# The order of the three products of a split matrix multiply: all column tiles in each pass

## The chip, the cores and the metric

The kernel runs on one core of a Trainium2 chip. TensorE (PE) multiplies, VectorE (DVE) and ScalarE (ACT) work elementwise, GpSimd (POOL) and SyncE (SP) issue most of the DMAs. The metric is the device time of one execution in microseconds; the timed runs are repeated, and their median counts.

## What is computed

Two transformer blocks over 256 tokens of width 2048, all in float32. The first has a sparse attention with compressed, selected and windowed keys and a gated feed-forward layer; the second has a sliding-window attention beside a latent attention, a squared-ReLU feed-forward layer, and scales and shifts that come from a vector `c`. Cut to the products with large weights:

```
h = rmsnorm(x);  proj = h @ nsa_w_in;  x = x + attention(proj) @ nsa_w_out
z = rmsnorm(x) @ ffn_w_in;  x = x + (silu(z[:, :5632]) * z[:, 5632:]) @ ffn_w_out;  x = rmsnorm(x)
mod = silu(c) @ w_mod + b_mod          # six vectors: sh1, sc1, g1, sh2, sc2, g2
h = rmsnorm(x) * (1 + sc1) + sh1;  proj = h @ w_in   (also w_uq, w_ukv)
x = x + g1 * (concat(window(proj), latent(proj)) @ w_out)
h = rmsnorm(x) * (1 + sc2) + sh2
x = x + g2 * (relu(h @ w_ff1) ** 2 @ w_ff2);  return rmsnorm(x)
```

## The kernel before

**Tiles and splitting.** Activations lie feature-major, 16 tiles `xs` of 128 features by 256 tokens (`S`). Each float32 value is split into a high half (rounded to the engine's fp32r form) and a low half, the rest: `split` (L83) has ACT write the high half (L84) and DVE the low half (L85). An activation tile holds both, `xt[:, 0, :]` high and `xt[:, 1, :]` low; they are made by `scaled` (L672 on ACT, L673 on DVE), `modulated` (L931, L933, L934) or `split`. A product of two split numbers is three products on TensorE: high x high, high x low, low x high (`mm3`, L125 to L129, weights first). The weights are the stationary operand, x the moving one, 256 columns wide.

**`gemm` (L131)** multiplies a block of weight columns by all x tiles. The columns are `nm` tiles of 128; each has half a PSUM bank, so a bank (`acc`, four of them in turn) holds two column tiles. Weights come in pieces of `kk` x tiles (`w_cols`): SP loads a piece into `raw` (five buffers), ACT and DVE split it into `whi` and `wlo` (four buffers each). The loop runs over the pieces, over the x tiles k of a piece, and over the column tiles m, and for each m writes the three products one after the other. At the end `evac` empties the banks: L642 adds to `h` (two tiles of `h` at once), L1086 does the same with a scale, one tile at a time. `gemm_tok` (L153) and `gemm_tok2` (L192) are the token-major forms with the weights as the moving operand; they have their own products.

**How wide.** Most gemms are 512 columns wide (`nm` = 4, two banks). `nsa_w_out` (L1036) runs as two gemms of eight column tiles, four banks each. `w_out_2` (L1092) runs as gemms of 8, 4, 2, 1 and 1 column tiles (`WIDE`), and the last part of `ffn_w_out` of 4, 4, 4, 2, 1 and 1 (`GROUPS`).

**What sets the order.** The code is written in program order, and a scheduler lays out each engine's instructions by its own estimate of when operands are ready. Attention heads are written between gemms, so their small matmuls (names `S`, `PT`, `O`; L588 to L629 in the first block, L952 to L1006 in the second) come to stand among the products of the gemm beside them. The vector `mod` is worked out on DVE in the background (`macc`, L742, a step after each piece; four one-row matmuls at L723), with its loads `mw` on POOL's queue, paced by the product that was written last (`self.last`).

Of the kernel before, what the change touches and what calls it, by code (L numbers as in the profile page):

```python
# [17 lines left out]
S = 256  # L18
# [48 lines left out]
class Kernel:  # L67
# [63 lines left out]
    def gemm(self, w, ld, row, xs, cols, evac, kk=2, order=None):  # L131


        n = sum(c for _, c in cols)
        nm, nk = n // 128, len(xs)
        acc = [self.bank("acc", 4) for _ in range((nm + 1) // 2)]
        order = order or list(range(0, nk, kk))
        done = 0
        for k0 in order:
            c = min(kk, nk - k0)  # L140
            hi, lo = self.w_cols(w, ld, row + 128 * k0, c, cols)
            for k in range(c):
                xt = xs[k0 + k]
                done += 1
                for m in range(nm):
                    self.mm3(acc[m // 2][:, (m % 2) * S:(m % 2 + 1) * S],
                             hi[:, k, m * 128:(m + 1) * 128], lo[:, k, m * 128:(m + 1) * 128],
                             xt[:, 0, :], xt[:, 1, :], done == 1 and m % 2 == 0, done == nk)
            self.step(c * nm / 64)
        for i, b in enumerate(acc):  # L150
            evac(i, b)
# [1040 lines left out]
```

## Time and profile before

| what | us |
|---|---|
| median of the timed runs | 2122.26 |
| fastest and slowest of the three | 2120.37, 2122.82 |
| the profiled execution | 2119.85 |
| its span, first to last instruction | 2118.0 |
| PE busy | 2094.1 |
| weight loads (PEld) busy | 1992.5 |
| DVE busy | 1452.0 |
| ACT busy | 1017.1 |

The profiled execution is one of its own, so its span is not the span of a timed run. PE's products are pipelined: one lasts 0.28 us from its start to its end, and the next starts before it has ended. The busy time of PE is the union of these, so it says that PE had something in it and not how fast products followed each other; that is read from the starts in the timeline, or from the number of products in a stretch. A stretch counts each instruction that overlaps it. Stages by time: norm, projections and compressed keys to about 200 us, the first attention to 357, `nsa_w_out` to 420, the first feed-forward layer to 1150, the second block's projections and attention to 1355, `w_out_2` to 1400, the second feed-forward layer to the end.

### The profile page before, as it was taken

The page shows a single profiled execution, that of the slowest core. Times are in us where ns is not written, and L with a number is a line of the kernel's source. Part 1 is how long each engine was busy: PE and PEld are TensorE (multiplying, and loading weights), DVE is VectorE, ACT ScalarE, POOL GpSimd, SP SyncE. Part 2 cuts the span into 40 slices and gives each one's busy share as a digit, 9 for nine tenths or more (in the row PEclk, how much of TensorE's full clock was granted, in tenths as well). Part 3 has the DMA queues.
Part 4 walks back from the last instruction along what each step waited for, and adds up shares of the span by engine and source line. Part 5 has one row for each costly group of instructions (what it writes and reads, how often), then busy time and mean ns, then how long its engine had stood idle before and what let it go on. Part 6 is the DMA issues. An engine that isn't in the chain of part 4 may idle for free. (4 is left out here: it accounts for less than half of the span.)

```text
span 2118.0 us, 40943 instructions
## 1 busy us (share of the span) xinstructions
PE 2094.1 (99%) x16405; PEld 1992.5 (94%) x16405; DVE 1452.0 (69%) x2144; ACT 1017.1 (48%) x1504; POOL 162.9 (8%) x297
## 2 busy tenths in 40 slices
PE   9999999999999999999999999999999999999998
PEld 8899999999999999999999999899889989989987
DVE  7467876787777777877867676677676555555556
ACT  6334655554434434443445465565434534534543
POOL 2211000010110111101000000000100000000000
PEclk9999999999999999999999999999999999999999
DMA  8778555889889888888975663568887656656663
GB/s 277 261 234 311 170 163 180 286 265 296 276 282 303 274 301 281 279 294 276 298 233 156 182 183 112 160 196 280 283 294 233 194 191 194 193 193 193 192 194 133
DMA packets 288302, 492.29 MB, mean 232 GB/s; under 512 B 27111, under 2 KB 139338, under 8 KB 287856
## 3 DMA queue, kind: packets, MB, share of 16 engines
q1 hardware_dynamic: 254128, 371.20, 55.2%
q0 software_dynamic: 33408, 117.70, 16.7%
q8 instruction: 128, 2.10, 0.4%
q10 hardware_dynamic: 576, 0.79, 0.1%
q14 instruction: 62, 0.51, 0.1%
HBM read 487.21 MB, written 2.20 MB: 231 GB/s over the span
## 5 line engine op out<-in xcount | busy, mean ns | idle before, releaser
L84 ACT ACTIVATE whi<-raw 128x1024 fp32r<-128x1024 f32 (+2 forms) x716 | 746.2, 1044 | 904.8 <-PE acc L128 645.4
L85 DVE TENSOR_TENSOR wlo<-raw,whi 128x1024 fp32r<-128x1024 f32 (+2 forms) x716 | 853.5, 1200 | 392.1 <-ACT whi L84 378.8
L127 PE MATMUL acc<-x,whi 128*128 128x256 f32 x3184 | 882.6, 278 | 3.2 <-ACT v L463 1.4
L128 PE MATMUL acc<-x,whi 128*128 128x256 f32 x3184 | 884.3, 278 | 0.0
L129 PE MATMUL acc<-x,wlo 128*128 128x256 f32 x3184 | 882.7, 278 | 0.2 <-DVE wlo L85 0.2
L127 PEld LDWEIGHTS acc<-x,whi 128*128 128x128 f32 x3184 | 597.8, 188 | 8.6 <-issue 5.0
L128 PEld LDWEIGHTS acc<-x,whi 128*128 128x128 f32 x3184 | 599.4, 188 | 5.4 <-issue 4.6
L129 PEld LDWEIGHTS acc<-x,wlo 128*128 128x128 f32 x3184 | 599.0, 188 | 1.4 <-DVE wlo L85 0.6
L742 DVE SCALAR_TENSOR_TENSOR macc<-mw,csil,macc 128x1024 f32<-128x1024 f32 x180 | 231.1, 1284 | 175.0 <-DMA mw<-w_mod 174.1
L128 PE MATMUL acc<-u,whi 128*128 128x256 f32 x1260 | 349.7, 279 | 0.8 <-DVE u L85 0.8
L127 PE MATMUL acc<-u,whi 128*128 128x256 f32 x1260 | 346.3, 280 | 1.0 <-DVE h L642 0.6
L129 PE MATMUL acc<-u,wlo 128*128 128x256 f32 x1260 | 347.0, 278 | 0.0
L128 PEld LDWEIGHTS acc<-u,whi 128*128 128x128 f32 x1260 | 236.7, 188 | 1.9 <-DVE u L85 1.5
L127 PEld LDWEIGHTS acc<-u,whi 128*128 128x128 f32 x1260 | 234.9, 188 | 3.2 <-ACT u L84 1.0
L129 PEld LDWEIGHTS acc<-u,wlo 128*128 128x128 f32 x1260 | 235.9, 188 | 0.7 <-issue 0.2
L164 PE MATMUL acc<-whi,u 128*128 128x512 f32 (+1 forms) x544 | 206.2, 379 | 0.0
L165 PE MATMUL acc<-wlo,u 128*128 128x512 f32 (+1 forms) x544 | 206.1, 379 | 0.0
L163 PE MATMUL acc<-whi,u 128*128 128x512 f32 (+1 forms) x544 | 204.4, 376 | 0.0
L736 POOL DMA_DIRECT2D mw<-w_mod x192 | 102.6, 534 | 1003.2 <-PE acc L129 657.7
L164 PEld LDWEIGHTS acc<-whi,u 128*128 128x128 f32 x544 | 102.2, 188 | 20.6 <-issue 0.4
L163 PEld LDWEIGHTS acc<-whi,u 128*128 128x128 f32 x544 | 102.1, 188 | 20.3
L165 PEld LDWEIGHTS acc<-wlo,u 128*128 128x128 f32 x544 | 102.2, 188 | 18.4
(349 smaller groups left out, 1316.9 us busy)
## 6 DMA issues: line engine op xcount, KB each, us to landing
raw<-w_ff SPq DMA_DIRECT2D x256, 512.0 KB, 4.1
mw<-w_mod POOLq DMA_DIRECT2D x192, 512.0 KB, 5.6
raw<-ffn_w_in SPq DMA_DIRECT2D x352, 256.0 KB, 5.0
raw<-ffn_w_out SPq DMA_DIRECT2D x87, 512.0 KB, 5.3
raw<-nsa_w_in SPq DMA_DIRECT2D x72, 512.0 KB, 5.3
raw<-nsa_w_out SPq DMA_DIRECT2D x32, 512.0 KB, 4.5
raw<-w_out SPq DMA_DIRECT2D x32, 512.0 KB, 4.0
raw<-w_in SPq DMA_DIRECT2D x24, 512.0 KB, 3.9
```

Source lines behind the costliest of these rows:

```text
L84: self.nc.scalar.activation(hi, x, AF.Copy)
L85: self.nc.vector.tensor_tensor(lo, x, hi.bitcast(F32), OP.subtract)
L127: mm(out, wh, xh, start=first, stop=False, skip_group_check=True)
L128: mm(out, wh, xl, start=False, stop=False, skip_group_check=True)
L129: self.last = mm(out, wl, xh, start=False, stop=last, skip_group_check=True)
L163: mm(o, xt[:, 0, q], hi, start=k == 0, stop=False)
L164: mm(o, xt[:, 1, q], hi, start=False, stop=False)
L165: self.last = mm(o, xt[:, 0, q], lo, start=False, stop=k == nk - 1)
L736: ld = nc.gpsimd.dma_start(wt, self.src(self.a["w_mod_2"], k * 128 * LD + s * 1024, [[LD, 128], [1, 1024]]))
L742: nc.vector.scalar_tensor_tensor(acc, wt, csil[:, k:k + 1], acc, op0=OP.mult, op1=OP.add)
```

## The change

The loop over column tiles moves inside a loop over the three passes. For one x tile, the first pass runs high weights x low x over all column tiles, the second high x high, the third low x high. The order of the three is other than before (high x high was first). The first product of a bank still opens it, the last pass of the last x tile closes it. `gemm_tok` and `gemm_tok2` stay as they are, and so does `mm3`, which `w_ukv` still calls. Names of lines from here on are two higher in the changed kernel (L642 is L644 there), and all the moved products have line L147.

```
-                for m in range(nm):
-                    self.mm3(acc[m // 2][:, (m % 2) * S:(m % 2 + 1) * S],
-                             hi[:, k, m * 128:(m + 1) * 128], lo[:, k, m * 128:(m + 1) * 128],
-                             xt[:, 0, :], xt[:, 1, :], done == 1 and m % 2 == 0, done == nk)
+                for i, (wt, j) in enumerate(((hi, 1), (hi, 0), (lo, 0))):
+                    for m in range(nm):
+                        self.last = self.nc.tensor.matmul(
+                            acc[m // 2][:, (m % 2) * S:(m % 2 + 1) * S], wt[:, k, m * 128:(m + 1) * 128], xt[:, j, :],
+                            start=done == 1 and i == 0 and m % 2 == 0, stop=done == nk and i == 2,
+                            skip_group_check=True)
```

PE in the first attention, around the transposes of one head (`PT` from `sb_2326`; `O` is the head's output). Before:

```order
L129 MATMUL acc<-x,wlo 128x256
L127 MATMUL acc<-x,whi 128x256
L620 MATMUL PT<-ident,sb_2326 128x128 x4
L128 MATMUL acc<-x,whi 128x256
L129 MATMUL acc<-x,wlo 128x256
L127 MATMUL acc<-x,whi 128x256
L626 MATMUL O<-pt,vcc 128x256
L128 MATMUL acc<-x,whi 128x256
L129 MATMUL acc<-x,wlo 128x256
```

The same place in the changed kernel:

```order
L147 MATMUL acc<-x,wlo 128x256 x4
L147 MATMUL acc<-x,whi 128x256 x8
L622 MATMUL PT<-ident,sb_2326 128x128 x4
L628 MATMUL O<-pt,vcc 128x256
L147 MATMUL acc<-x,wlo 128x256 x4
L147 MATMUL acc<-x,whi 128x256 x8
```

The eight products of the two high passes now stand together and the four low ones behind them; the three products between the head's two steps have moved away from there, so that the gemm is broken into once and not twice.

DVE at the end of the first gemm of `nsa_w_out`, where the four banks are added to `h` and the next x tiles are scaled. Before:

```order
L742 SCALAR_TENSOR_TENSOR macc<-mw,csil,macc 128x1024
L85 TENSOR_TENSOR wlo<-raw,whi 128x1024
L642 TENSOR_TENSOR h<-h,acc 128x512
L85 TENSOR_TENSOR wlo<-raw,whi 128x1024
L742 SCALAR_TENSOR_TENSOR macc<-mw,csil,macc 128x1024
L642 TENSOR_TENSOR h<-h,acc 128x512 x2
L673 SCALAR_TENSOR_TENSOR x<-h,vec_821,x 128x256
L642 TENSOR_TENSOR h<-h,acc 128x512
L673 SCALAR_TENSOR_TENSOR x<-h,vec_821,x 128x256
```

The same place in the changed kernel:

```order
L744 SCALAR_TENSOR_TENSOR macc<-mw,csil,macc 128x1024
L85 TENSOR_TENSOR wlo<-raw,whi 128x1024 x2
L744 SCALAR_TENSOR_TENSOR macc<-mw,csil,macc 128x1024
L644 TENSOR_TENSOR h<-h,acc 128x512 x4
L85 TENSOR_TENSOR wlo<-raw,whi 128x1024
L675 SCALAR_TENSOR_TENSOR x<-h,vec_821,x 128x256 x2
```

The four additions, which stood among a weight split, a `macc` step and a scaling, now stand in one row behind the `macc` step.

## Rows read from the trace of the kernel before

**Rows 1.** The page's head and busy times: us, share of the span, instructions.
```profile
span 2118.0 us, 40943 instructions
...
PE 2094.1 (99%) x16405; PEld 1992.5 (94%) x16405; DVE 1452.0 (69%) x2144; ACT 1017.1 (48%) x1504; POOL 162.9 (8%) x297
```

**Rows 2.** Waits of PE: who waited for whom, us in total, times, longest.
```profile
PE acc L127 <- DVE h L642: 1.3, 2, 0.7
...
PE acc L128 <- DVE u L85: 0.8, 2, 0.7
...
PE acc L129 <- DVE wlo L85: 0.2, 1, 0.2
```

**Rows 3.** Timeline of PE, feed-forward stretch: start us, duration us, instruction.
```profile
500.29 0.28 PE L127 MATMUL acc<-x,whi 128*128 128x256 f32 x1
500.40 0.28 PE L128 MATMUL acc<-x,whi 128*128 128x256 f32 x1
500.51 0.28 PE L129 MATMUL acc<-x,wlo 128*128 128x256 f32 x1
500.63 0.28 PE L127 MATMUL acc<-x,whi 128*128 128x256 f32 x1
```

**Rows 4.** PE in stretches: stretch, length, PE busy (instructions), granted clock, DMA share, GB/s.
```profile
460.00:530.00 70.00, 70.00 (x620) 1.00 0.92 299
...
1357.00:1397.00 40.00, 40.00 (x342) 1.00 0.61 180
```

**Rows 5.** The page's costliest groups: count | busy us, mean ns | idle before.
```profile
L128 PE MATMUL acc<-x,whi 128*128 128x256 f32 x3184 | 884.3, 278 | 0.0
...
L128 PE MATMUL acc<-u,whi 128*128 128x256 f32 x1260 | 349.7, 279 | 0.8 <-DVE u L85 0.8
```

**Rows 6.** Timeline, DVE and PE, middle of `nsa_w_out`; in brackets the idle time before.
```profile
376.60 1.28 DVE L742 SCALAR_TENSOR_TENSOR macc<-mw,csil,macc 128x1024 f32<-128x1024 f32 x1 [1.14 <-DMA mw<-w_mod]
...
377.63 0.28 PE L128 MATMUL acc<-u,whi 128*128 128x256 f32 x1
377.80 1.28 DVE L642 TENSOR_TENSOR h<-h,acc 128x512 f32<-128x512 f32 x2
...
378.54 0.39 PE L127 MATMUL acc<-u,whi 128*128 128x256 f32 x1 [0.63 <-DVE h L642]
```

**Rows 7.** Timeline, DVE and PE, end of `nsa_w_out`.
```profile
419.92 0.68 DVE L642 TENSOR_TENSOR h<-h,acc 128x512 f32<-128x512 f32 x1
...
420.75 0.36 PE L127 MATMUL acc<-x,whi 128*128 128x256 f32 x1 [0.67 <-DVE h L642]
```

**Rows 8.** Timeline of DVE, end of the eight-wide gemm of `w_out_2`.
```profile
1353.79 3.23 DVE L1086 SCALAR_TENSOR_TENSOR h<-acc,modc,h 128x256 f32<-128x256 f32 x8 [0.95 <-PE acc L129]
```

**Rows 9.** Timeline of PE at the same place.
```profile
1355.23 0.28 PE L129 MATMUL acc<-u,wlo 128*128 128x256 f32 x1
...
1355.38 0.36 PE L127 MATMUL acc<-u,whi 128*128 128x256 f32 x1
```

**Rows 10.** Timeline, first gemm of the second block's projections.
```profile
1154.25 0.80 PE L127 MATMUL acc<-x,whi 128*128 128x256 f32 x2 [1.12 <-ACT x L933]
...
1154.89 0.58 PE L128 MATMUL acc<-x,whi 128*128 128x256 f32 x1
```

**Rows 11.** Timeline, first gemm of the second feed-forward layer.
```profile
1406.77 0.49 PE L127 MATMUL acc<-x,whi 128*128 128x256 f32 x2
...
1407.28 0.38 PE L128 MATMUL acc<-x,whi 128*128 128x256 f32 x1
```

**Rows 12.** Timeline of PE, products after a break in the first attention.
```profile
304.74 0.47 PE L129 MATMUL acc<-x,wlo 128*128 128x256 f32 x1
305.05 0.28 PE L127 MATMUL acc<-x,whi 128*128 128x256 f32 x1
```

**Rows 13.** Timeline of PE at the lower clock, first gemm of the kernel.
```profile
9.54 0.41 PE L128 MATMUL acc<-x,whi 128*128 128x256 f32 x1
...
10.18 0.41 PE L129 MATMUL acc<-x,wlo 128*128 128x256 f32 x1
```

## The prediction, made before the changed kernel ran

> **What bounds the kernel now.** I read the page's head first: the span is 2118.0 us, PE is busy 2094.1 us of it, DVE 1452.0 and ACT 1017.1 [rows 1]. So TensorE is the bound from end to end, and a busy share of 99% may still hide a poor pace. The waits come next, and PE hardly has any: two waits for a bank come to 1.3 us, two for a low half to 0.8, one for `wlo` to 0.2 [rows 2]. The weights' splits are always early. Then the pace itself. In the feed-forward stretch the timeline shows one product starting every 0.113 us, whatever follows what: L127 to L128 (same output, same weights, the other half of x), L128 to L129 (same output, other weights), L129 to L127 (other output, other weights, same half of x) [rows 3]. Over whole stretches the counts say the same. A stretch counts about two instructions more than start in it, because a product lasts 0.28 us and those begun earlier count too: 70 us / 618 = 113.3 ns, but 40 / 340 = 117.6, both at full granted clock [rows 4]. So there are two paces, 113.3 and 117.7 ns. By the starts in the timeline the slow one holds four long stretches (38.3 to 59.4, 172.9 to 189.9, 1355.6 to 1400.6, 1583.1 to 1597.6 us, some 830 products) and about as many again in short pieces of the attention stages: 1,650 x 4.4 ns = 7.3 us. The lines that the change touches make 3 x (3184 + 1260) = 13,332 products [rows 5]; one nanosecond on each would be 13.3 us.
>
> **The steady part: 0.** Nothing is removed or added: the same 13,332 products, with as many weight loads, over the same operands. What changes is which product follows which. Of the new neighbours, "other output, other weights, same half of x" makes ten of twelve steps with four column tiles; in the other two the half or the tile of x changes as well. It stands in the trace before as L129 to L127, at 0.113 us like the two others [rows 3]. The weights of a column tile were loaded twice in a row before (L127, L128) and are loaded four loads apart now; the trace shows no saving on the second of the two, so none is lost. I take 0, and the two paces as the bounds of what can happen (rivals below). `hi` is read to the end earlier and `lo` is needed later, by six products (0.7 us) in a piece of four tiles. ACT and DVE get that as slack; it is worth the one `wlo` wait, -0.2 us [rows 2].
>
> **Where the sum is: the ends of gemms eight tiles wide.** Before, the column tiles of the last k finish one after the other, three products each, so a bank (two tiles) is done every 0.68 us and DVE can empty it while PE works on. Now all tiles finish in the third pass, and the four banks are done 0.23 us apart, the first only six products before the end. The next gemm takes the same four banks, and now asks for all of them within its first pass. There are three such places.
> (a) Inside `nsa_w_out`, first to second half. Before, the last bank's add is late because DVE does `macc` first (376.60, 1.28 us) and then adds of 0.64 us; PE waits once, from about 377.85 to 378.54 [rows 6]. In the new order the four adds stand in a row behind `macc`. From 377.88 they end at 378.5, 379.1, 379.8 and 380.4; the first pass then ends near 380.7, not at 378.76 as without a wait: 1.9 us lost against 0.7, so +1.2. Were `macc` not in front, the adds begin at 377.4 and it is +0.75.
> (b) `nsa_w_out` to the feed-forward's first gemm, which takes two banks. Before, PE waits for the first (419.92 to 420.75) [rows 7]; now the second ends 0.64 us after the first while its turn comes 0.23 us after: +0.4 (0.2 to 0.6).
> (c) `w_out_2`, eight tiles to four. Before, no wait: DVE's eight updates take 3.23 us from 1353.79, 0.40 each, two to a bank [rows 8], and PE goes straight from 1355.23 to 1355.38 [rows 9]. Now the first bank is done at 1355.23 - 6 x 0.118 + 0.28 = 1354.8 and is empty at 1355.65, the second at 1356.45: PE loses 0.3 and then 0.6 us: +0.9 (0.6 to 1.2). The gemms of one and two tiles after it take other banks or end as before.
> Elsewhere two of the four banks serve a gemm of four tiles, and the next one takes the other two: a later release is hidden behind a whole gemm, and would cost up to 0.45 us per gemm without that.
>
> **The low half of x comes first now.** ACT writes the high half of an activation, DVE the low half after it. Before, PE could start with high x high. At 1154.25 and at 1406.77 it does two products so and then waits for DVE's L934 until 1154.89 and 1407.28 [rows 10, 11]. Now the first product waits for that: two products at 0.11 to 0.28 us each, 0.4 us each time, +0.8 together (0.4 to 1.2). In the second attention PE's order before has eleven places where four products of L127 run ahead of the low half. Each could cost up to 4 x 0.113 = 0.45 us, 5.0 us in all, or nothing where other matmuls fill it. Only two waits for `u`'s low half stand in the trace [rows 2], so I take two of them, +1.0 (0 to 5.0).
>
> **The order around it.** The scheduler moves the attention's small matmuls too. Counted over the whole of PE's order, runs of these products are broken into by other work 145 times before and 135 times now. A break shows its price where a product is followed after 0.31 us instead of 0.11 (304.74 to 305.05) [rows 12]: 0.2 us, and by the starts around other breaks 0.1 or hardly any. Ten fewer: -1.5 (-3.0 to 0). SP's queue keeps its order word for word, so no load moves.
>
> **Sum.** 0 - 0.2 + 1.2 + 0.4 + 0.9 + 0.8 + 1.0 - 1.5 = +2.6 us. The profiled execution took 2119.85 us (its span plus 1.85), so this gives 2122.45 for it; the median of the timed runs is 2122.26, and with the same 2.6 us on it the forecast is **2124.9 us**, 0.12% longer. With all terms at their low or high ends it is 2121.0 to 2131.5. About 0.2%, 4.2 us, is what a measurement of this kernel can tell from no change, so the bounds are 2118.0 and 2126.5.
>
> **Rivals.**
> 1. *The slow pace holds more of the products* (slower). Where: after each break the first products run at 117.7 ns, and something later drops PE to 113.3; in four long stretches it did not. If the new sequence of loads and products never drops out, the price is 4.4 ns x 11,700 = 51 us, 2176 us; a quarter of that gives 2138. It decides from some 360 products more than now (1.6 us to the bound). For: both paces come from something in the rhythm that the order could touch. Against: within each pace all three neighbours cost alike.
> 2. *PE's clock falls because the bank changes at every second product* (slower). Row first: from 460 to 530 us the bank changes at every sixth product and the granted clock is 1.00 [rows 4]; at the lower level products start 0.21 us apart (9.54 to 10.18) [rows 13]. The change triples the bank changes. If one product in twenty fell to the lower level, it would cost 667 x 0.1 = 67 us: 2192 us. The Trainium skill, "TensorE: Matmul & The Clock Gate", section "A second HAM failure mode: psum-queue depth-cycling", tells of a kernel that cycles through PSUM banks and whose clock swings between its levels, because PE idles a little between groups. By that rule this change would be slower; the trace so far speaks against it, since L129 to L127 changes the output without a gap.
> 3. *The slow pace goes away* (faster): -7.3 us on the sum, 2117.6.
> 4. *The waits at the starts do not arise*, because the scheduler fills them: without (a) to (c) and the low-half terms the sum is -1.7, 2120.6: no change that could be measured.
>
> **How the numbers follow.** Forecast 0.55 (within 0.2%: 0.38, slower 0.17); rival 1 0.12, slower; rival 2 0.04, slower; rival 3 0.17 (faster 0.10, same 0.07); rival 4 0.12 (same 0.10, faster 0.02). Together: faster 0.12, same 0.55, slower 0.33. The range 2114 to 2137 leaves out rival 2 (0.04), rival 1 beyond 8 us or so (0.08) and the far end of rival 3 (0.04).
>
> **What would show it.** In the new profile: products of the new line 113.3 ns apart in the feed-forward stretch, and counts per stretch that give 113.3 or 117.7 and nothing else; waits of PE for `h` of 1 to 2 us at the middle of `nsa_w_out` and some 0.9 us at the end of the eight-wide part of `w_out_2`; waits for the low half of x at the two stage starts; no wait for `wlo`. I am wrong if the pace in the long stretches is another number, if the granted clock falls inside them, or if the waits of PE grow by more than 6 us.

## The result, and the profile of the changed kernel

| | before | changed |
|---|---|---|
| median, us (12 runs each) | 2122.54 | 2133.22 |
| lowest to highest, us | 2119.65 to 2126.97 | 2127.50 to 2145.05 |
| profiled execution, us | 2119.85 | 2137.10 |
| its span, us | 2118.0 | 2135.2 |
| PE busy, us | 2094.1 | 2102.6 |

The changed kernel is slower: 1.0053 times the time of before, 95% interval 1.0041 to 1.0065, or some 11 us. That lies inside the range of 2114 to 2137, but outside the forecast's own case: +2.6 us was forecast, and "within 0.2%" was the likeliest sign. The profiled execution of the changed kernel is 4 us above its median; a second one (last experiment) took 2131.76 us, and I read both.

The page of the changed kernel: the head, the busy times, and the costliest groups of the new line (count | busy us, mean ns | idle us before it). They answer to [rows 1, 5].

```profile
span 2135.2 us, 40964 instructions
...
PE 2102.6 (98%) x16405; PEld 2001.0 (94%) x16405; DVE 1450.1 (68%) x2144; ACT 1016.3 (48%) x1504; POOL 163.0 (8%) x297
...
L147 PE MATMUL acc<-x,whi 128*128 128x256 f32 x6368 | 877.6, 279 | 5.7 <-ACT v L465 2.4
...
L147 PE MATMUL acc<-x,wlo 128*128 128x256 f32 x3184 | 502.7, 279 | 0.0
```

The instruction counts of the engines are those of before, so nothing was added. The new line waits 5.7 us where L127 waited 3.2. PE's waits in the changed kernel (us in total, times, longest), which answer to [rows 2]:

```profile
PE acc L147 <- DVE h L644: 2.8, 2, 1.6
PE acc L147 <- ACT v L465: 2.4, 1, 2.4
PE PT L967 <- DVE sb L964: 2.2, 2, 1.7
PE acc L147 <- DVE x L936: 2.1, 2, 1.8
PE S L725 <- DVE macc L744: 1.7, 3, 1.3
PE acc L147 <- DVE u L85: 1.7, 2, 0.9
```

Other lines of this list are left out. The same list of before has the waits for `h` (1.3), `v` (1.4), `sb` (0.7), `macc` (0.4) and `u` (0.8), and 1.1 for the high half of an activation where the low half stands now. The wait for `wlo` is gone. Added up between its first and last product, PE is idle 14.6 us before and 22.5 us after.

Two sums over PE's product starts explain most of the rest. Products at the slow pace (115 to 120 ns to the next) are 1731 before and 2901 now: 1170 x 4.4 ns = 5.1 us. Products at the lower of the two clock levels, 0.21 us apart [rows 13], are 23 before and 68 now: 45 x 0.1 = 4.5 us. Without these two, PE's busy time is 2094.1 - 7.6 - 2.3 = 2084.2 us before and 2102.6 - 12.8 - 6.8 = 2083.0 now. So 8.0 + 5.1 + 4.5 - 1.2 = 16.4 of the 17.2 us between the two spans; the other 0.8 stand behind PE's last instruction.

The slow pace is seen in stretches of the trace (stretch, its length, PE busy and instructions, granted clock, DMA share, GB/s). The changed kernel:

```profile
460.00:530.00 70.00, 70.00 (x620) 1.00 0.92 293
990.00:1084.00 94.00, 94.00 (x801) 1.00 0.87 277
```

The first has the count of before to the last product [rows 4]: the new order runs at 113.3 ns there. The second is 94 / 799 = 117.6 ns, in the same loop, with the granted clock at 1.00. Before, the same 94 us held 833 instructions.

### The profile page after: what moved, and what is told of

Read it like the earlier page. It is cut to its first block, busy times and chain, and to the rows that moved or that the text cites. A ratio compares the mean times of both kernels' runs of the same rounds, so it can differ in the third digit from the quotient of the medians.

```text
span 2135.2 us, 40964 instructions
## 1 busy us (share of the span) xinstructions
PE 2102.6 (98%) x16405; PEld 2001.0 (94%) x16405; DVE 1450.1 (68%) x2144; ACT 1016.3 (48%) x1504; POOL 163.0 (8%) x297
## 5 line engine op out<-in xcount | busy, mean ns | idle before, releaser
L147 PE MATMUL acc<-x,whi 128*128 128x256 f32 x6368 | 877.6, 279 | 5.7 <-ACT v L465 2.4
L147 PEld LDWEIGHTS acc<-x,whi 128*128 128x128 f32 x6368 | 796.7, 189 | 15.6 <-issue 11.4
L147 PE MATMUL acc<-x,wlo 128*128 128x256 f32 x3184 | 502.7, 279 | 0.0
L147 PEld LDWEIGHTS acc<-x,wlo 128*128 128x128 f32 x3184 | 427.3, 189 | 1.1 <-issue 0.6
L147 PE MATMUL acc<-u,whi 128*128 128x256 f32 x2504 | 346.8, 279 | 3.4 <-DVE u L85 1.7
L147 PEld LDWEIGHTS acc<-u,whi 128*128 128x128 f32 x2504 | 313.9, 188 | 5.9 <-DVE u L85 2.4
L147 PE MATMUL acc<-u,wlo 128*128 128x256 f32 x1252 | 200.6, 278 | 0.0
L147 PEld LDWEIGHTS acc<-u,wlo 128*128 128x128 f32 x1252 | 168.6, 188 | 0.3
L578 ACT ACTIVATE sb<-sb,nm 128x128 f32<-128x128 f32 (+4 forms) x144 | 59.2, 413 | 35.8 <-DVE nm L575 35.6
L575 DVE CUSTOM_DVE_ANT_0 sb<-S,bt 128x128 f32<-128x128 f32 (+3 forms) x128 | 33.2, 308 | 3.4 <-PE S L986 1.3
```

Source lines behind the costliest of these rows:

```text
L147: self.last = self.nc.tensor.matmul(acc[m // 2][:, (m % 2) * S:(m % 2 + 1) * S], wt[:, k, m * 128:(m + 1) * 128], xt[:, j, :], start=done ...
L575: r = nc.vector.tensor_tensor_reduce(sb[:, c], s, b, 1.0, 3e38, OP.add, OP.min, nm[:, i:i + 1])
L578: nc.scalar.activation(sb[:, c], sb[:, c], AF.Exp, bias=nm[:, i:i + 1], scale=-1.0, accum_out=sums[:, i:i + 1])
```

## Experiments

Each has the median of its runs and its ratio to runs of before on the same chip, with the 95% interval. Line numbers in waits move with each edit. Theory A: the loss stands at the ends of gemms, where banks are finished together and the next gemm asks at once for all of them and for the low half. Theory B: it stands in the inner order, by way of the slow pace. Theory C, from experiment 5 on: any new order costs in proportion to how much it moves. Theories D, E, P and Q, on the slow pace, stand in the expectations of experiments 9 to 11.

**1. Both ends undone.** The changed kernel, with the first and last x tile of each gemm in the old order:

```diff
+                if done in (1, nk):
+                    for m in range(nm):
+                        self.mm3(acc[m // 2][:, (m % 2) * S:(m % 2 + 1) * S],
+                                 hi[:, k, m * 128:(m + 1) * 128], lo[:, k, m * 128:(m + 1) * 128],
+                                 xt[:, 0, :], xt[:, 1, :], done == 1 and m % 2 == 0, done == nk)
+                    continue
                 for i, (wt, j) in enumerate(((hi, 1), (hi, 0), (lo, 0))):
```

> The changed kernel with the first and the last x tile of every gemm back in the old order (three products for a column tile, then the next tile, high x high first); all x tiles between keep the three passes. Theory A (the loss is at the ends of gemms: banks released late, low half of x asked for first, and the lower clock that follows such gaps): PE idle between its first and last product back from 22.5 us to about 15, no wait for h over 0.8 us, time as before, ratio 0.999 to 1.0015. Theory B (the order inside the gemm holds more products at the slow pace of 117.7 ns): about 2900 products at that pace as in the changed kernel against 1730 before, +5 us, ratio 1.002 to 1.004.

Measured: 2121.8 us, 1.001 [0.9994, 1.0026]. The loss is gone, as far as this interval can tell, with the passes still in all x tiles between. PE's idle time in the profile is 16.0 us; one wait for `h` of 1.4 us stayed, where I had expected none over 0.8.

**2. The ends alone.** The complement: `if 1 < done < nk:` in the place of `if done in (1, nk):`.

> The complement: only the first and the last x tile of every gemm run in three passes, all between in the old order. Theory A: nearly the whole loss, PE idle about 22 us, waits for h of 1 to 2 us, at the lower clock 5 to 10 us more than before, ratio 1.003 to 1.005. Theory B: idle may grow, but the slow pace stays at about 1700 products, ratio 1.001 to 1.0025.

Measured: 2131.3 us, 1.0046 [1.003, 1.0062]: nearly the whole loss from the two end tiles of each gemm. PE's idle time is 23.9 us and 1477 products are slow, fewer than before. Theory B, that the inner order sets the loss, falls with these two.

**3. High half first.** The changed kernel with the first two passes exchanged:

```diff
-                for i, (wt, j) in enumerate(((hi, 1), (hi, 0), (lo, 0))):
+                for i, (wt, j) in enumerate(((hi, 0), (hi, 1), (lo, 0))):
```

> The changed kernel with the passes in the order high x high, high x low, low x high. Theory A: the waits for the low half of x and u (2.1 and 1.7 us in the changed kernel) go or halve, the waits for h stay, so 2 to 3 us less than the changed kernel, ratio 1.003 to 1.004. Theory B: the passes are as long as before, ratio 1.005 as the change, some 2900 products at the slow pace.

Measured: 2128.6 us, 1.0033 [1.0022, 1.0043]. PE's wait for the low half at the second block's first gemm became the old one of 1.1 us for the high half; the waits for `h` stayed at 3.0 us. The passes cost some 7 us without the low half's help. In this one profile, whose time is that of the median, little of it is idle time (17.1 us, 2.5 more than before) and more is the slow pace (3688 products, 8.6 us more).

**4. Low half first, in the old order.** The kernel before, with the first two products of `mm3` exchanged:

```diff
-        mm(out, wh, xh, start=first, stop=False, skip_group_check=True)
-        mm(out, wh, xl, start=False, stop=False, skip_group_check=True)
+        mm(out, wh, xl, start=first, stop=False, skip_group_check=True)
+        mm(out, wh, xh, start=False, stop=False, skip_group_check=True)
```

> The kernel before with only the order of the three products changed: high x low first, then high x high, then low x high, for each column tile. Theory A: waits for the low half come in, the banks are released as before: +1 to +2 us, ratio 1.0005 to 1.001. Theory B: no pass over all tiles, so no more slow products (1700), ratio 0.9995 to 1.0005.

Measured: 2126.95 us, 1.0031 [1.0017, 1.0045], more than I expected. The profile has 19.9 us of idle time and only 1188 slow products. Experiment 7 gives another answer to the same question, below.

**5 and 6. By width.** The three passes only in gemms of eight column tiles (`if nm < 8:` takes the old order), and only in the others (`if nm == 8:`).

> The kernel before with the three passes in the gemms of eight column tiles alone (four banks); the narrower gemms keep their old order. Theory A (the loss stands at the ends of gemms: banks that come free 0.23 us apart, a first pass that wants the low half and all banks at once, and a lower clock after the longer gaps): only the places behind eight-wide gemms lose, that is the middle and end of nsa_w_out and the boundary of w_out_2: +2 to +4 us, ratio 1.001 to 1.002, and the waits for h grow to 3 to 4 us while those for v, x and sb stay as they were before. Theory C (the amount of changed order counts, not the place): these gemms hold about a fifth of the products, so +2 us, ratio 1.001, and no wait stands out.

> The complement: three passes in all gemms but those of eight column tiles. Theory A: the waits for h stay at 1.3 us; those for v at the start of the q gemms, for the low half of x at two stage starts, for u and sb in the second attention grow as in the changed kernel: +6 to +9 us, ratio 1.003 to 1.004. Theory C: four fifths of the loss, +9 us, ratio 1.004. The two differ by which waits of PE are long.

Measured: 2128.8 us, 1.0038 [1.0026, 1.005], and 2127.2 us, 1.003 [1.0015, 1.0045]. The waits fall in the main as theory A said: `h` 5.0 us and `v` 1.3 in the first, `h` 1.5, `v` 2.1 and the low half of x 2.1 in the second, where only `u`'s low half didn't grow. The second's size is the expected one. The first's isn't: the eight-wide gemms alone cost twice what I gave them. Theory C wanted 1.001 of the first, below its interval. The two together, 3.8 and 3.0 thousandths, are more than the 5.3 of the full change, but not beyond what the three intervals allow. What stood in front of the adds to `h` at the end of `nsa_w_out` (experiment 5, timeline of DVE, start and duration in us, idle time in brackets):

```profile
422.61 1.28 DVE L750 SCALAR_TENSOR_TENSOR macc<-mw,csil,macc 128x1024 f32<-128x1024 f32 x1 [2.33 <-DMA mw<-w_mod]
423.81 1.22 DVE L85 TENSOR_TENSOR wlo<-raw,whi 128x1024 fp32r<-128x1024 f32 x1
424.95 1.28 DVE L650 TENSOR_TENSOR h<-h,acc 128x512 f32<-128x512 f32 x2
```

DVE stood idle for a load of `w_mod` for 2.33 us, with `macc` at the head of its queue, a weight split behind it, and the emptying of the banks behind both. So what a late bank costs hangs on when that load lands and on what stands between.

**7 and 8. One end each.** The changed kernel with only the last x tile in the old order (`if done == nk:`), and with only the first (`if done == 1:`).

> The changed kernel with the last x tile of each gemm in the old order, column tile by column tile, so that the banks come free 0.68 us apart again; the first x tile still begins with the low half. Theory A: what is left is the low half first and its clock stretches, about what it cost alone in the old order: +4 to +7 us, ratio 1.002 to 1.003; waits for h near 1.5 us, for v about 2.4 us. If the late banks are the whole loss: ratio 1.000 to 1.001.

> The changed kernel with the first x tile of each gemm in the old order, so that the high half is used first and the second, third and fourth bank are asked for 0.68 us apart; the last x tile still ends in three passes, its banks 0.23 us apart. Theory A: waits for the low half gone; a bank that is freed late is also asked for later, so the waits for h fall to 2 us or less: +2 to +5 us, ratio 1.001 to 1.0025. If the low half first is the whole loss: ratio 1.000 to 1.001. If the late banks are: about 1.003 as with the high half first.

Measured: 2123.5 us, 1.0004 [0.9991, 1.0017], and 2130.0 us, 1.0038 [1.0023, 1.0054]. The last tile decides. With banks 0.68 us apart again nothing is lost that can be measured, though the low half still comes first; with the first tile mended and the last not, 8 us stay. My theory A had expected 1.002 to 1.003 of the first, because of experiment 4, and 1.001 to 1.0025 of the second, with waits for `h` of 2 us or less; they are 3.4 us there. Even in experiment 7 the profile has one wait for `h` of 3.0 us, at the end of `nsa_w_out`, behind a `macc` that waited 2.85 us for its load; in the middle, where the changed kernel lost 1.58, there is none. This profile took 2126.91 us, the second longest of the 12 runs; its idle time is 19.3 us, still 4.7 more than before.

**9 and 10. The pace by itself.** Four small matmuls (eight instructions in the trace) behind each of the 56 gemms of both feed-forward stages break the run of products. Once with the inner order of before, once with the new one:

```diff
+        if self.breaks:
+            p = self.bank("S", 2)
+            for j in range(4):
+                i = self.nc.tensor.matmul(p[:, 128 * j:128 * j + 128], self.ident, self.ident, start=True, stop=True)
+                self.hold(i, [self.last])
         for i, b in enumerate(acc):
             evac(i, b)
```

> The kernel before, with four small matmuls (identity by identity, never read) added behind each of the 56 gemms of both feed-forward stages, so that the run of products is broken 56 times there. At each break the pace may be chosen anew, 113.3 or 117.7 ns. The four matmuls cost 0.5 to 0.7 us each time, 28 to 40 us in all. Theory D (the pace behind a break is a draw, and the inner order weights it): few or none of the segments between breaks are slow here, under 1 in 20 of the products, as in the kernels with the old inner order so far. Theory E (the draw does not depend on the inner order): the same share of slow segments as in the twin kernel with the new order.

> The changed kernel with the same four small matmuls behind each of the 56 gemms of both feed-forward stages. Theory D (the inner order weights the draw): a tenth or more of the products between the breaks at 117.7 ns, 700 products or more, 3 us or more beyond the twin kernel with the old order. Theory E: the share of the twin kernel, and a time that differs from the twin's only by the ends of gemms, 6 to 11 us.

Measured: 2171.8 us, 1.0246 [1.0232, 1.026], and 2184.6 us, 1.0306 [1.0292, 1.032]. Stretches between two breaks, old inner order first and then the new (columns as above):

```profile
828.00:848.00 20.00, 20.00 (x172) 1.00 0.81 257
920.00:940.00 20.00, 20.00 (x172) 1.00 0.71 228
1018.00:1038.00 20.00, 20.00 (x178) 1.00 0.95 303
```

```profile
832.00:852.00 20.00, 20.00 (x172) 1.00 0.83 269
925.00:945.00 20.00, 20.00 (x173) 1.00 0.77 245
1018.00:1038.00 20.00, 20.00 (x172) 1.00 0.79 255
```

172 instructions in 20 us is 117.6 ns, 178 is 113.6. Of the 54 segments between two breaks inside the feed-forward stages, 4 are slow with the old order and 6 with the new, one of these in part; all four of the old ones are at the same place in the program in the new kernel. So the pace is set anew at each break, in the segments seen it goes on to the next one, and both orders get it at mostly the same places. In products of these slow segments that is 651 of 8983 and 985 of 8986, where theory D wanted under 1 in 20 for the old order and, in time, 3 us more for the new. D finds little support: 334 products more, 1.5 us. Of the 13.3 us between the spans of the two profiles 5.8 is idle time, as theory E said of the ends of gemms; 5.0 is slow pace, most of it outside the feed-forward stages, and 3.9 the lower clock. The whole, 12.8 us between the medians, is a little more than E's 6 to 11. A break cost 49.9 / 56 = 0.89 us, where I had put 0.5 to 0.7.

**11. The changed kernel a second time.**

> The changed kernel itself, profiled a second time. If the places of the slow pace belong to the program (theory P), the stretches of the first profile are slow again: 380 to 447 us and 990 to 1084 us, some 2900 products at 117.7 ns in all. If they are drawn anew at each execution (theory Q), other stretches are slow and the count moves by several hundred, and the time by 4.4 ns for each. The waits of PE at the ends of gemms stay in both: for h 2.8 us, for v 2.4, for the low half of x 2.1.

Measured: 2131.76 us, one run. PE's idle time is 22.6 us again, the slow products are 2879, those at the lower clock 23 as before the change. The first profile had 22.5, 2901 and 68. Two stretches of the second profile:

```profile
990.00:1084.00 94.00, 93.32 (x829) 1.00 0.89 290
...
455.00:546.00 91.00, 91.00 (x775) 1.00 0.87 279
```

The stretch at 990 us was slow in the first profile and is at full pace here; the one at 455 us is slow here (91 / 773 = 117.7 ns) and was not (809 instructions then). That is theory Q. But the stretch behind the middle of `nsa_w_out`, from 380 us on, is slow both times, as theory P said. The 45 more products at the lower clock are not in the second execution, so the change doesn't bring them each time.

**12. High half first, and the last tile in the old order.** Experiment 3 with the lines of experiment 7.

> The changed kernel with both parts of its ends undone in another way: the passes begin with high by high, and the last x tile of each gemm is computed column tile by column tile. If banks that come free together are the loss (theory A, as it stands after the last runs): ratio 0.999 to 1.001. If the three passes at the start, which ask for all banks within a few products, cost by themselves: 1.001 to 1.002. If any new order of the attention's small matmuls costs as much as was seen (theory C): about 1.003.

Measured: 2123.2 us, 1.0002 [0.9984, 1.002]. Three passes at a gemm's start cost nothing that can be measured. Theory C, which wanted 1.003 here, falls. Its profiled execution was the fastest of its 12 runs (2114.3 to 2127.8), as was that of experiment 1; so I read no gain from their profiles.

## Why the prediction was right and wrong

**The steady part: right.** The new neighbours run at 113.3 ns (460 to 530 us), and in experiments 1, 7 and 12 the passes over the inner x tiles cost nothing that can be measured. PE's busy time without slow pace and lower clock fell by 1.2 and 2.0 us in the two profiles, which fits the -1.5 of the ten fewer breaks.

**The middle and end of `nsa_w_out`, (a) and (b): right in size, wrong in the step.** Timeline of DVE and then of PE in the changed kernel, which answers to [rows 6, 7]:

```profile
378.27 1.28 DVE L744 SCALAR_TENSOR_TENSOR macc<-mw,csil,macc 128x1024 f32<-128x1024 f32 x1 [0.69 <-DMA mw<-w_mod]
379.59 2.48 DVE L644 TENSOR_TENSOR h<-h,acc 128x512 f32<-128x512 f32 x4
...
425.17 1.22 DVE L85 TENSOR_TENSOR wlo<-raw,whi 128x1024 fp32r<-128x1024 f32 x1
426.31 1.88 DVE L644 TENSOR_TENSOR h<-h,acc 128x512 f32<-128x512 f32 x3
```

```profile
377.78 1.07 PE L147 MATMUL acc<-u,wlo 128*128 128x256 f32 x8
380.42 0.71 PE L147 MATMUL acc<-u,whi 128*128 128x256 f32 x4 [1.58 <-DVE h L644]
...
427.13 0.71 PE L147 MATMUL acc<-x,whi 128*128 128x256 f32 x4 [1.25 <-DVE h L644]
```

The four adds stand in a row behind `macc`, as the step said. PE waits 1.58 us (1.87 in the second profile) instead of 0.63, and 1.25 (1.26) instead of 0.67: +0.95 to +1.24 and +0.58, against +1.2 and +0.4. But the step let the last bank decide at (a) and the second at (b), because the next gemm "asks for all of them within its first pass". It doesn't. In the order that the scheduler laid out for PE, the next gemm computes 22 products on its first bank at (a), and 23 at (b), before it touches the second; the kernel before does the same with 20 and 25. At (a) the second bank is asked for at 383.09, 2.2 us after its add has ended. So PE waits for one add alone, the first, and the rest of the row costs nothing. Before, the first bank was free when PE came to it at 375.47, and the wait of [rows 6] was for the second; now the first is finished only with the others (its last product ends at 378.17) and DVE has other work in front: `macc`, which waits for its load, at (a), and a weight split at (b). Experiment 5 shows what both can cost. That the sum of these came out near the forecast is luck.

**`w_out_2`, (c): wrong, +0.9 forecast, some 0.2 measured.** Timeline of DVE and of PE, which answers to [rows 8, 9]:

```profile
1371.74 3.23 DVE L1088 SCALAR_TENSOR_TENSOR h<-acc,modc,h 128x256 f32<-128x256 f32 x8 [2.41 <-PE acc L147]
```

```profile
1371.31 1.07 PE L147 MATMUL acc<-u,wlo 128*128 128x256 f32 x8
1372.28 0.33 PE L1105 MATMUL O<-ident,h 128*128 128x128 f32 x1
1372.67 0.74 PE L147 MATMUL acc<-u,whi 128*128 128x256 f32 x4
1373.24 0.39 PE L147 MATMUL acc<-u,wlo 128*128 128x256 f32 x2
```

DVE was idle when the first bank was ready and had its two updates done by 1372.61. PE had a transpose to do and went on at 1372.67, 0.06 us after its end; the next four products took 0.12 us more than the 0.62 that four take at full pace. The second bank's 0.6 us of the forecast could not arise: four products with high weights and two with low ones are one x tile of two column tiles, that is of one bank, though the gemm has four tiles. PE asks for its second bank only after 25 products, at 1375.62, and DVE had freed it at 1373.40. This is rival 4 at one place: the scheduler's order fills the wait.

**The low half at the stage starts: right in size.** Idle time at 1165.45 us is 1.84 instead of the 1.12 in [rows 10]. Before, the two products in front lost time too that counts as busy; up to the gemm's 25th product 0.4 us of the difference are left in the second profile. At the second start PE now idles 0.26 us, of which 0.2 are left by the same count.

**The second attention, +1.0 of a range to 5.0: mis-sized, +3.2 us in both profiles.** Two groups of waits grew. Up to 1298 us they are 1.82 us before and 3.68 now; the largest is new (PE, then DVE, which stands in front):

```profile
1297.68 0.74 PE L967 MATMUL PT<-ident,sb 128*128 128x128 f32 x3 [1.69 <-DVE sb L964]
```

```profile
1295.66 0.16 DVE L962 RECIPROCAL sums<-sums 128x2 f32<-128x2 f32 x1
...
1295.85 1.23 DVE L85 TENSOR_TENSOR wlo<-raw,whi 128x1024 fp32r<-128x1024 f32 x1
1296.99 0.54 DVE L964 TENSOR_SCALAR sb<-sb,sums 128x256 f32<-128x256 f32 x2
```

The softmax's last step stands behind a weight split of 1.23 us. The product order moved, the scheduler placed the attention's small work otherwise, and a split now falls between two steps of a softmax. The second group, at the last heads before `w_out_2`, went from 1.13 us (157 + 304 + 670 ns) to 2.51; most of it is `u`'s low half. Here my step asked only for the low half of x and for banks, and it held that elsewhere "a later release is hidden behind a whole gemm". It is, as a bank. But a result that is finished later also reaches the scores, the softmax and the transposes later, and those have no gemm to hide behind. That sentence is the step that failed here. The trace shows the wait and its queue; that the lateness of the result is what moved the split there is inferred from experiments 1, 7 and 12, in whose profiles PE has no wait for this `sb` at all.

**Not in the sum.** The wait for `macc` at its column sums: 0.4 us before, 1.7 and 2.3 in the two profiles, though it is as large in experiment 1, which loses nothing. The wait for `v` at 174.29 us: 2.39 us in one profile and 1.39 in the other, against 1.40 before.

**Rival 1, the slow pace, came true in small.** I gave it 0.12, with 51 us if it took all, and a point of decision at 360 products more; both profiles have some 1,160 more, 5.1 us. Experiments 9 to 11 say what it is not: the rhythm of the new sequence alone does not fix it. It is set at breaks and waits. In the two profiles it holds the second half of `nsa_w_out` (behind the grown wait of (a)) and one or another segment of the feed-forward layer; but in experiment 10's profile that half, behind a wait of 2.17 us, runs at 113.4 ns over 368 products, so the wait doesn't force it. **Rival 2 was wrong:** with the bank changing at every second product the granted clock is 1.00 from 460 to 530 us. The Trainium skill, "TensorE: Matmul & The Clock Gate", section "A second HAM failure mode: psum-queue depth-cycling", speaks of a clock that swings where a kernel cycles through banks, and puts it down to short idle times of PE between groups; here no idle time came with the cycling, and no swing.

**The account.** In the second profile, the one near the median: +8.0 us idle, +5.1 slow pace, -2.0 order, 0 clock: 11.1 of the 11.9 us between the spans. The forecast had +4.1 of waits and -1.5. By the prediction's own sign, waits that grow by more than 6 us, it was wrong, although the time lies in its range: they grew by 7.9 and 8.0. What failed in the sum is the slow pace taken as 0 (5.1 short), the second attention (2.2 short) and the unpriced wait for `macc` (1.9 short in this profile), against 0.7 too much for `w_out_2`: 8.5 us, from 2.6 to 11.1. Two sentences failed in the steps: that the next gemm asks for all banks within its first pass, which made (c) too dear and left (a) and (b) right by luck only, and that elsewhere a later release is hidden behind a whole gemm. The place that I put at the centre, the last x tile, whose banks come free together, is the one that decides: undoing it alone (experiment 7) takes 10 us off. By what road the whole 10 us come from the late banks is not shown: only 3.2 and 3.3 us of idle time lie between the two profiles of the changed kernel and that of experiment 7, and in experiment 3's most of the loss is slow pace. I counted waits at three places; what a wait sets off behind it had no term.

**Open.** Experiments 4 and 7 both put the low half first without late banks, and measure 1.0031 [1.0017, 1.0045] and 1.0004 [0.9991, 1.0017]; the profiles of both have the same idle time (19.9 and 19.3 us). I can't say which holds for the low half alone: some 1 or some 7 us by the medians. The kernel before was profiled once, so how far its 1731 slow products move from one execution to the next isn't known, nor then how much of the 5.1 us is the change's. What makes PE take one pace or the other behind a break stays unknown, and a weight of the inner order on it is not excluded: over the profiles of before and experiments 2, 4 and 5, where most products have the old order, 1188 to 1790 products are slow, and over the changed kernel's two and experiments 1, 3, 6, 7, 8 and 12, where most have the new one, 1403 to 3688. (In experiments 5 to 8 single starts scatter more, and some 400 to 550 products of the full pace fall among the slow ones.)

## What to carry to other kernels

A loop order that leaves TensorE's steady pace untouched can still cost at the ends of a reduction: there it sets when each bank is finished, and one behind the other was better here than all together, for the next gemm's first bank and, as argued above, for whoever reads the results. If an order is wanted for the inner steps, keep the last step tile by tile; in these runs that gave the loss back as far as could be measured. Read in the scheduler's order, and not in the code's, when a gemm asks for its second bank. And price a wait on a busy TensorE with what comes behind it: the queue of the engine that empties the bank, a load at its head, and the pace after the break.

## What the runs showed of the hardware

- The same loop runs at 113.3 or at 117.6 ns a product, at full granted clock, for as long as no break comes: 94 us with 801 instructions in one execution, with 829 in another of the same kernel. The Trainium skill, "TensorE: Matmul & The Clock Gate", section "Back-to-back issue gap", has a formula for the isolated gap of a single matmul at the higher clock, N/2.4 + 2.5 ns, an estimate of 109 ns for 256 columns; both paces here, with a weight load for each product, lie above it.
- Loading the same weights twice in a row, as L127 and L128 did, saves nothing against loading them four loads apart: 113.3 ns both ways, over the same 70 us with 620 instructions each.
- Four small matmuls (eight instructions) in the run of products cost 0.89 us at each of 56 places, with whatever follows them.
